# Ten running sums kept as halves: five in PSUM, five through three rotating banks, and a dot product that writes over its row

## The chip, the cores and the metric

The kernel runs on one core of a Trainium2 chip. The metric is device time in microseconds (us), the median of several runs. On the core, TensorE (PE in the profile) multiplies matrices and writes the products to PSUM, whose eight banks each hold a tile of 128 x 512 float32. VectorE (DVE) and ScalarE (ACT) read PSUM and SBUF, GpSimd (POOL) issues the indirect DMAs that fetch rows, and SyncE (SP) issues the others. Each engine runs its own instructions in order and waits on semaphores for the others.

## The reference

One layer of a diffusion backbone over 128 prompt tokens and 1024 sample tokens of width 1024, nine token tiles of 128 in all: norm, a mixer with a spatial gate and a two-way recurrence, a residual, and then PEER retrieval, where this change lies. Cut to that:

```python
def peer(x, w_q, sub_keys, u_tab, v_tab):        # 8 heads, 2 x 128 keys, 128*128 experts
    s = einsum('thpc,hpkc->thpk', q, sub_keys)   # scores of the two key halves
    ...                                          # 16 best of each half, 16 best sums of a head
    idx, g = chosen experts (128 a token), softmax over each head's 16
    a = gelu(einsum('bd,bed->be', x, u_tab[idx])) * g
    return einsum('be,bed->bd', a, v_tab[idx])
x = x + gate2 * peer(h, ...)                     # then a last norm and the store
```

## The kernel before

The first 1.78 ms norm the tokens, run the mixer in groups of token tiles, work out the experts of every token, and write a weight matrix G to DRAM for five of the tiles. The rest is retrieval, done in two ways at once.

**Dense.** The five tiles of `DENSE` (640 tokens) meet all 16384 experts, in 128 expert tiles of 128 (the loop over `e`). For one expert tile, `hidden` multiplies `u` with the tokens in two halves of 320 columns (`pH`, 24 matmuls each: 8 steps of the contraction, three products of split operands), ScalarE applies gelu into `a`, VectorE multiplies by G (`Gt`, line 1062), and the pair `split` makes `aH`, `aL` (line 99 on ScalarE, line 100 on VectorE). `u` and `v` are loaded and split in the same way. Then `a` times `v` is added to the sums, ten blocks of 128 tokens by 512 columns, three matmuls a block. Six blocks (three token tiles, `RES`) have a PSUM bank each for the whole loop and are added up there (`pout`, `out_res`). The other four (`ROT` = 2 tiles) are multiplied only after every fourth expert tile (`GI` = 4), for the four together (`prot`, `out_rot`: 12 matmuls a block); VectorE then adds the block to an SBUF sum `accd` (line 1045). 32 such groups make up the loop.

**Row by row.** The tiles of `GATHER` get their 128 chosen rows a token by indirect DMA. `gather` takes a row of `u` into a slot (`gu`), multiplies it by the token's vector with a running sum (line 798: the product goes to a scratch tile `jk`, the sum to `dots`), and after 16 of them fetches 16 rows of `v` (`gv`) and adds them up, weighted, in `acc` (line 813). This work fills VectorE beside the dense loop: `fill` is called after each split and each sum, advances `gather` by a fixed rate, and ties the new instructions behind an earlier one of the dense work (`anchor`, `paced`). The late choice of experts of a tile (`combine_late`, tile names `late`, `cmp`, `prod`) is filled in the same way.

PSUM is two rings: `pmm` (tag `mm`, six banks) and `ptp` (tag `tp`, two banks). A ring hands its banks out in the order of the code, so a new tile waits until the reader of the tile that had the bank before has finished. `pH`, `prot` and, before the dense loop, transposes, squares (`sqj`), the one-hot products of the G build (`pG`) and others all come from `tp`. What order an engine's instructions stand in is decided by a scheduler when the kernel is built; the code gives the dependencies.

At the end `final` multiplies a tile's sum by the gate, adds the residual, norms and stores it.

Of the kernel before, what the change touches and what calls it, by code (L numbers as in the profile page):

```python
# [20 lines left out]
NT = 9            # token tiles of 128: tile 0 is the prompt, 1..8 the sample  # L21
NS = 8
EPS = 1e-6
CF = {}           # slots of [128, 512] and of [128, 1024] in the pool of a phase
NGR = 4           # slots of fetched rows, and those that the dense pass adds
# [7 lines left out]
AH = (1, 2)       # of how many blocks of one-hots ScalarE does the weighting  # L33
# [4 lines left out]
TB = 32           # tokens of a block of the weight matrix in DRAM  # L38
OT = 4            # tokens of a block of one-hots
GI = 4            # expert tiles of one load of the weights  # L40
# units of 128 x 1024 weights in the stream
U_ZI, U_HG, U_GR = 0, 4, 16
GATHER = [0, 1, 2, 3]                             # token tiles whose experts are fetched row by row
DENSE = [5, 6, 7, 8, 4]                           # token tiles that meet every expert
ND = len(DENSE)
TD = 128 * ND
RES = 3                                           # dense tiles whose sums stay in PSUM
ROT = ND - RES


@with_exitstack
def hybrid_kernel(ctx, tc, x_all, pos, c2t, w_ada, b_ada, wst, wspt, bsp, lbraw, vecs, fng, skt, state,
# [8 lines left out]
    def pmm(name="pmm"):  # L61
        return psum.tile([128, 512], F32, name=name, tag="mm", bufs=6)

    def ptp(name="ptp"):
        return psum.tile([128, 512], F32, name=name, tag="tp", bufs=2)
# [3 lines left out]
    gate_d = dram.tile([4, D], F32, name="gate_d")      # gate1 (ctx, lat), gate2 (ctx, lat)  # L69
# [12 lines left out]
    vec = consts.tile([128, 24], F32, name="vec")        # g1(8) g2(8) sgu(4) hgrn(4), channel on partition  # L82
# [6 lines left out]
    lb = consts.tile([128, 3, 8], F32, name="lb")        # lb, (1-lb)/2, (1+lb)/2  # L89

# [13 lines left out]
    def anchor(ins, keep):  # L104
        """the filling work on VectorE queues behind the main stream's instruction `keep` anchors ago"""
        anchors.append(ins)
        while len(anchors) > keep:
            anchors.popleft()
# [15 lines left out]
    def mmx(ps, a, b, first, last):  # L124
        """a.T @ b for operands in one float32 part or in two float32r parts"""
# [10 lines left out]
    def rap(t, off, dims):  # L136
        """free-dim pattern on a tile"""
        a = t[:]
        return bass.AP(tensor=a.tensor, offset=a.offset + off, ap=[list(a.ap[0])] + dims)

# [9 lines left out]
    # work that fills the engines beside the main stream: generators, advanced a step at a time  # L150
# [42 lines left out]
    # order of the six modulation vectors: shift1 scale1 gate1 shift2 scale2 gate2  # L193
# [30 lines left out]
    def norm_T(pool, xn, which, cnd, parts, back=None):  # L224
        """transposes normalised tiles, applies scale and shift, stores the parts; back(k, full) sees
        the whole float32 value"""
# [41 lines left out]
    def proj_rows(u0, opd, n, evac, native, half=None):  # L268
        """token-major product with a 512 wide block (4 units); opd(k): parts [128, T]; evac(i, psum)"""
# [16 lines left out]
    def hgrn(pool, blocks, proj, vsrc, states):  # L286
        """blocks: (token tile, head) of each 128 columns; proj(j, evac): products for q, fw, bw"""
        NB = len(blocks)
        NTOK = NB * 128
        K2 = pool.tile([128, 2, NTOK], F32, name="K2")       # fw, bw  # L290
        Q2 = pool.tile([128, 2, NTOK], F32, name="Q2")       # bw, fw
        F2 = pool.tile([128, 2, NTOK], F32, name="F2")       # fw, bw
# [27 lines left out]
        for lev in range(7):  # L320
            w = 1 << lev
            Kc = pool.tile([128, NTOK], F32, name="Kc", bufs=1)   # even segments forward, odd ones backward
# [11 lines left out]
            # K: fw first halves by the total of the second, bw second halves by the total of the first  # L334
# [8 lines left out]
            # totals of the doubled segments: the second level in T2, the others in place of the gates  # L343
# [7 lines left out]
        T128 = tbase                                        # F2[:, d, T128 + block]  # L351
# [63 lines left out]
    def combine(gp, t, tv, ti, al=None, c4=None, V=V, h0=0, h1=8, res=None):  # L415
        """the 16 best sums of a head: products of the two lists, with (i+1)(j+1) <= 16"""
        if al is None:
            def al(name, n, dt=F32):
                return gp.tile([128, n], dt, name=name, bufs=1)
# [25 lines left out]
        if res is None:  # L445
            res = al("res", 384).rearrange("p (a b) -> p a b", a=3)    # i1, i2, g
# [3 lines left out]
        hk = lambda x: x[:, :, None, :].to_broadcast(SH)                     # over the list position  # L450
        lp = lambda x: x[:, :, :, None].to_broadcast(SH)                     # over the chosen
# [26 lines left out]
        # softmax over the 16 of a head  # L478
# [16 lines left out]
        else:  # L495
# [3 lines left out]
            rt = gp.tile([128, 2, 128], F16, name="rt", bufs=4)      # i2, i1  # L499
            V.tensor_copy(rt, pt[:, 0:256].rearrange("p (a b) -> p a b", a=2))  # L500
            rg = gp.tile([128, 128], F32, name="rg", bufs=4)         # g (scaled)
            V.tensor_scalar(rg, pt[:, 256:384], 16384.0, None, op0=OP.mult)
            gl = gp.tile([128, 2, 128], F16, name="gl", bufs=4)      # its float16 part, what is left
# [4 lines left out]
    def build_G(gp, i, rt, rg, gl, tags):  # L508
        SH = [128, 2, 128, OT]

        def one_hots(t0):
            o4 = gp.tile([128, 4, 128 * OT], F16, name="oh", tag="c4", bufs=3)
            oh = o4[:, 0:2].rearrange("p a (j t) -> p a j t", t=OT)          # of i2, of i1
# [673 lines left out]
```

## Time and profile before

| | |
|---|---|
| three runs | 3690.14, 3692.68, 3700.58 us |
| median | 3692.68 us |
| profiled execution | span 3697.6 us; the page gives no other time for it |
| PE busy in the span | 3351.2 us (91%) |
| VectorE busy | 2840.2 us (77%) |
| ScalarE busy | 1157.4 us (31%) |
| GpSimd busy | 1440.8 us (39%) |
| dense loop, first to last `pout` or `prot` | 1784.3 to 3674.2 us of the span |

The span reaches from the first to the last instruction. Matmuls overlap, each beginning before the one ahead of it has ended, so how fast PE goes is read from one start to the next, and its idle time from the rows that name a wait.

### The profile page before, as it was taken

To read this page: it belongs to the slowest core of one execution; us is meant where nothing else is said; L and a number is where in the kernel's file an instruction comes from. 1 tells how busy PE (TensorE), PEld (TensorE's weight loads), DVE (VectorE), ACT (ScalarE), POOL (GpSimd) and SP (SyncE) were. 2 spreads that over 40 slices of the span, in tenths; PEclk is the share of its full clock that TensorE was granted. 3 is DMA by queue.
4 is the path that set the end of the run, shared out by engine and by line. 5 is a ranking of instruction groups with operands and counts; after the bars stand their busy time and mean duration, and the time that the engine had idled before them with its cause. 6 is when DMAs were issued, how large, how long until landed. Compare 5 with 4: busy or idle time off the path is not lost. (4 is left out here: it accounts for less than half of the span.)

```text
span 3697.6 us, 48818 instructions
## 1 busy us (share of the span) xinstructions
PE 3351.2 (91%) x17547; PEld 2757.2 (75%) x17547; DVE 2840.2 (77%) x5427; ACT 1157.4 (31%) x2075; POOL 1440.8 (39%) x1128
## 2 busy tenths in 40 slices
PE   7787889899797899888789999889999989999997
PEld 3265678777476676576688989788888878898996
DVE  1315698787499987588787889888888888888888
ACT  2511233432222387735322222222222222222222
POOL 0100632265311220000255554556555465655664
PEclk9899999999898999888799999999999999999998
DMA  7676854488842476441798898889988799989986
GB/s 267 226 272 208 297 189 153 158 292 307 296 161 97 163 278 252 172 165 75 257 327 307 316 335 286 311 298 330 326 308 316 256 327 338 318 301 328 328 313 249
DMA packets 361957, 971.12 MB, mean 263 GB/s; under 512 B 32721, under 2 KB 142673, under 8 KB 356081
## 3 DMA queue, kind: packets, MB, share of 16 engines
q0 software_dynamic: 149824, 546.37, 41.6%
q1 hardware_dynamic: 211888, 421.62, 33.1%
q8 instruction: 138, 2.26, 0.2%
q14 instruction: 107, 0.87, 0.1%
HBM read 897.07 MB, written 70.80 MB: 262 GB/s over the span
## 5 line engine op out<-in xcount | busy, mean ns | idle before, releaser
L795 POOL DMA_INDIRECT gu<-in_urow_dram,ix x512 | 693.5, 1354 | 1024.8 <-DVE jk L798 368.8
L808 POOL DMA_INDIRECT gv<-in_vrow_dram,ix x512 | 694.7, 1357 | 720.6 <-DVE acc L813 388.2
L798 DVE SCALAR_TENSOR_TENSOR jk<-gu,h2r 128x1024 f16<-128x1024 f32 x512 | 624.9, 1220 | 125.0 <-DMA gu<-in_urow_dram,ix 118.7
L813 DVE SCALAR_TENSOR_TENSOR acc<-gv,act,acc 128x1024 f32<-128x1024 f32 x508 | 651.3, 1282 | 65.9 <-DMA gv<-in_vrow_dram,ix 57.9
L129 PE MATMUL pH<-h2DH,uH 128*128 128x320 f32 x2016 | 626.1, 311 | 11.3 <-DVE accd L1045 10.4
L131 PE MATMUL pH<-h2DH,uL 128*128 128x320 f32 x2016 | 623.6, 310 | 3.4 <-DVE uL L100 3.4
L130 PE MATMUL pH<-h2DL,uH 128*128 128x320 f32 x2016 | 624.2, 310 | 0.0
L129 PEld LDWEIGHTS pH<-h2DH,uH 128*128 128x128 f32 x2016 | 380.5, 189 | 21.8 <-DVE accd L1045 15.6
L130 PEld LDWEIGHTS pH<-h2DL,uH 128*128 128x128 f32 x2016 | 380.3, 189 | 4.4
L131 PEld LDWEIGHTS pH<-h2DH,uL 128*128 128x128 f32 x2016 | 380.1, 189 | 4.3 <-DVE uL L100 4.3
L129 PE MATMUL pout<-vH,aH 128*128 128x512 f32 x768 | 298.5, 393 | 22.6 <-ACT vH L99 16.3
L99 ACT ACTIVATE vH<-vr 128x1024 fp32r<-128x1024 f32 x128 | 133.3, 1058 | 561.4 <-DMA vr<-in_vrow_dram 289.4
L130 PE MATMUL pout<-vL,aH 128*128 128x512 f32 x768 | 301.1, 392 | 6.2 <-DVE vL L100 6.2
L131 PE MATMUL pout<-vH,aL 128*128 128x512 f32 x768 | 300.4, 391 | 1.1 <-DVE aL L100 1.0
L129 PE MATMUL prot<-vH,aH 128*128 128x512 f32 x512 | 211.7, 414 | 57.8 <-DVE accd L1045 51.8
L99 ACT ACTIVATE wH<-wraw 128x1024 fp32r<-128x1024 f32 x118 | 125.1, 1060 | 439.4 <-PE pq L130 148.4
L100 DVE TENSOR_TENSOR vL<-vr,vH 128x1024 fp32r<-128x1024 f32 x128 | 156.0, 1220 | 93.7 <-ACT vH L99 93.6
L99 ACT ACTIVATE aH<-a 128x640 fp32r<-128x640 f32 x128 | 94.2, 736 | 368.5 <-DVE a L1062 363.7
L130 PE MATMUL prot<-vL,aH 128*128 128x512 f32 x512 | 208.0, 406 | 0.0
L131 PE MATMUL prot<-vH,aL 128*128 128x512 f32 x512 | 207.3, 405 | 0.0
L99 ACT ACTIVATE uH<-ur 128x1024 fp32r<-128x1024 f32 x126 | 133.4, 1058 | 234.1 <-PE pH L130 214.5
L543 PE MATMUL pG<-oh 128*128 128x128 f16 x1280 | 159.4, 281 | 35.0 <-ACT Gs L546 20.3
(343 smaller groups left out, 6407.7 us busy)
## 6 DMA issues: line engine op xcount, KB each, us to landing
wraw<-in_wst_dram SPq DMA_DIRECT2D x216, 512.0 KB, 4.4
vr<-in_vrow_dram SPq DMA_DIRECT2D x128, 512.0 KB, 6.4
ur<-in_ut_dram SPq DMA_DIRECT2D x126, 512.0 KB, 6.8
G_d<-Gs SPq DMA_DIRECT2D x40, 1024.0 KB, 4.1
Gt<-G_d SPq DMA_DIRECT2D x160, 256.0 KB, 8.7
wraw<-in_w_ada_dram SPq DMA_DIRECT2D x48, 512.0 KB, 4.4
gu<-in_urow_dram,ix POOLq DMA_INDIRECT x512, 6.3
gv<-in_vrow_dram,ix POOLq DMA_INDIRECT x512, 6.9
```

Of the source, the lines that this page charges most:

```text
L99: A.activation(H, src, AF.Copy)
L100: return V.tensor_tensor(out=L, in0=src, in1=H.bitcast(F32), op=OP.subtract)
L129: P.matmul(ps, a[0], b[0], start=first, stop=False)
L130: P.matmul(ps, a[0], b[1], start=False, stop=False)
L131: P.matmul(ps, a[1], b[0], start=False, stop=last)
L543: P.matmul(pg[:, tt * 128:(tt + 1) * 128], oh[:, 0, :, tt], og[a][:, :, tt], start=(a == 0), stop=(a == 1))
L795: G.indirect_dma_start(out=ur, out_offset=None, in_=urow, in_offset=bass.IndirectOffsetOnAxis(ap=ix[:, c:c + 1], axis=0))
L798: paced(V.scalar_tensor_tensor(jk, ur, 1.0, h2r, op0=OP.mult, op1=OP.mult, accum_out=dots[:, k:k + 1]))
L808: G.indirect_dma_start(out=vr, out_offset=None, in_=vrow, in_offset=bass.IndirectOffsetOnAxis(ap=ix[:, c:c + 1], axis=0))
L813: paced(V.scalar_tensor_tensor(acc, vr, act[:, k:k + 1], acc, op0=OP.mult, op1=OP.add))
```

## The change

PSUM's eight banks are cut five and three in place of six and two: `mm` gets five, `tp` three. The unit of a sum becomes a half tile. The first five halves stay in PSUM (two tiles and the left half of the third), five rotate, and `accd` is five tiles of 128 x 512 in place of two of 128 x 1024. A group thus has 15 `pout` matmuls an expert tile (18 before), 60 `prot` matmuls (48 before) and five sums on VectorE (four before). The rate of `fill` is divided by 3 x 4 + 5 = 17 calls a group in place of 16, so that a group still fetches 24.4 rows. The final takes a tile's sum as two halves for all five tiles, into a `ftmp` tile each. The product of line 798 goes back over the fetched row in float32, and the scratch tile `jk` (float16) is gone. Comments are dropped, which moves line numbers by one or so.

```diff
-RES = 3
-ROT = ND - RES
+RES = 5
+ROT = 2 * ND - RES
...
-        return psum.tile([128, 512], F32, name=name, tag="mm", bufs=6)
+        return psum.tile([128, 512], F32, name=name, tag="mm", bufs=5)
...
-        return psum.tile([128, 512], F32, name=name, tag="tp", bufs=2)
+        return psum.tile([128, 512], F32, name=name, tag="tp", bufs=3)
...
-                jk = gat.tile([128, D], F16, name="jk", bufs=1)
-                paced(V.scalar_tensor_tensor(jk, ur, 1.0, h2r, op0=OP.mult, op1=OP.mult,
+                paced(V.scalar_tensor_tensor(ur, ur, 1.0, h2r, op0=OP.mult, op1=OP.mult,
                                              accum_out=dots[:, k:k + 1]))
...
-    po = [[pmm("pout") for _ in range(2)] for _ in range(RES)]
-    accd = [dp.tile([128, D], F32, name=f"accd{i}") for i in range(ROT)]
+    halves = [(i, n) for i in range(ND) for n in range(2)]
+    po = [pmm("pout") for _ in range(RES)]
+    accd = [dp.tile([128, 512], F32, name=f"accd{i}") for i in range(ROT)]
...
-        advance(gather_q, RATE[4] * GI / (3 * GI + 2 * ROT))
+        advance(gather_q, RATE[4] * GI / (3 * GI + ROT))
...
+    def cols(i, n):
+        return slice(i * 128, (i + 1) * 128), slice(n * 512, n * 512 + 512)
...
+        for z in range(RES):
+            t, s = cols(*halves[z])
+            mmx(po[z], [aH[:, t], aL[:, t]], [vH[:, s], vL[:, s]], e == 0, e == 127)
...
+        for z in range(ROT):
+            t, s = cols(*halves[RES + z])
+            pr = ptp("prot")
+            for m, (_, aH, aL, vH, vL) in enumerate(grp):
+                mmx(pr, [aH[:, t], aL[:, t]], [vH[:, s], vL[:, s]], m == 0, m == len(grp) - 1)
+            if grp[0][0] == 0:
+                ins = V.tensor_copy(accd[z], pr)
+            else:
+                ins = V.tensor_tensor(out=accd[z], in0=accd[z], in1=pr, op=OP.add)
+            fill(ins)
...
+    sums = po + accd
...
-        final(dp, DENSE[i], dst, po[i] if i < RES else [dst], x1, gt2, fgd)
+        final(dp, DENSE[i], dst, sums[2 * i:2 * i + 2], x1, gt2, fgd)
```

The first place is VectorE's queue at the sums of one group in the middle of the dense loop, where the second row by row tile has just been finished. `jk` or `gu` is a product of line 798, `accd` a sum, and the waits in brackets are on DMAs (DMASW, DMAHW), PE, ScalarE (Activation), GpSimd (Pool) or VectorE's own last results (DVE). Before:

```order
L798 SCALAR_TENSOR_TENSOR jk_19331,dots_19318<-gu_19329,h2r_19315 128x1024 [waits DMASW5_49]
L798 SCALAR_TENSOR_TENSOR jk_19335,dots_19318<-gu_19333,h2r_19315 128x1024 [waits DMASW6_49,DVE_49]
L1045 TENSOR_TENSOR accd0_13757<-accd0_13757,prot_19365 128x512 [waits PE_49]
L798 SCALAR_TENSOR_TENSOR jk_19345,dots_19318<-gu_19343,h2r_19315 128x1024 [waits DMASW7_49,DVE_49]
L1045 TENSOR_TENSOR accd0_13757<-accd0_13757,prot_19387 128x512 [waits PE_49]
L798 SCALAR_TENSOR_TENSOR jk_19381,dots_19318<-gu_19379,h2r_19315 128x1024 [waits DMASW2_49,DVE_49]
L798 SCALAR_TENSOR_TENSOR jk_19385,dots_19318<-gu_19383,h2r_19315 128x1024 [waits DMASW0_49,DVE_49]
L1045 TENSOR_TENSOR accd1_13758<-accd1_13758,prot_19405 128x512 [waits PE_49]
L798 SCALAR_TENSOR_TENSOR jk_19403,dots_19318<-gu_19401,h2r_19315 128x1024 [waits DMASW1_49,DVE_49]
L100 TENSOR_TENSOR vL_19524<-vr_19521,vH_19523 128x1024 [waits DMAHW5_49,Activation_49]
L798 SCALAR_TENSOR_TENSOR jk_19421,dots_19318<-gu_19419,h2r_19315 128x1024 [waits DMASW3_49,DVE_49]
L1045 TENSOR_TENSOR accd1_13758<-accd1_13758,prot_19427 128x512 [waits PE_49]
```

Four sums stand there with one or two products between them. The same place of the changed kernel:

```order
L797 SCALAR_TENSOR_TENSOR gu_19082,dots_19081<-gu_19082,h2r_19078 128x1024 [waits DMASW4_49]
L797 SCALAR_TENSOR_TENSOR gu_19085,dots_19081<-gu_19085,h2r_19078 128x1024 [waits DMASW5_49]
L1044 TENSOR_TENSOR accd0_13628<-accd0_13628,prot_19112 128x512 [waits PE_49]
L797 SCALAR_TENSOR_TENSOR gu_19126,dots_19081<-gu_19126,h2r_19078 128x1024 [waits DMASW7_49]
L797 SCALAR_TENSOR_TENSOR gu_19129,dots_19081<-gu_19129,h2r_19078 128x1024 [waits DMASW2_49,DVE_49]
L1044 TENSOR_TENSOR accd1_13629<-accd1_13629,prot_19132 128x512 [waits PE_49]
L797 SCALAR_TENSOR_TENSOR gu_19146,dots_19081<-gu_19146,h2r_19078 128x1024 [waits DMASW0_49]
L1044 TENSOR_TENSOR accd2_13630<-accd2_13630,prot_19149 128x512 [waits PE_49]
L797 SCALAR_TENSOR_TENSOR gu_19163,dots_19081<-gu_19163,h2r_19078 128x1024 [waits DMASW1_49]
L797 SCALAR_TENSOR_TENSOR gu_19166,dots_19081<-gu_19166,h2r_19078 128x1024 [waits DMASW3_49,DVE_49]
L1044 TENSOR_TENSOR accd3_13631<-accd3_13631,prot_19169 128x512 [waits PE_49]
```

The fifth sum follows one product later; the density of sums and products is about the same, and most products no longer wait on VectorE itself.

The second place is a little ahead of it in the changed kernel, where the products of one head are fetched. GpSimd issues the fetches in this order:

```order
L795 DMA gu_18478<-in_urow_dram,ix1_13750 128x1024
L795 DMA gu_18481<-in_urow_dram,ix1_13750 128x1024
L795 DMA gu_18563<-in_urow_dram,ix1_13750 128x1024
L795 DMA gu_18572<-in_urow_dram,ix1_13750 128x1024
L795 DMA gu_18581<-in_urow_dram,ix1_13750 128x1024
```

and VectorE works on them in this one (rows of other work between them included):

```order
L797 SCALAR_TENSOR_TENSOR gu_18563,dots_18371<-gu_18563,h2r_13752 128x1024 [waits DMASW3_49]
L100 TENSOR_TENSOR uL_18569<-ur_18566,uH_18568 128x1024 [waits DMAHW4_49,PE_49]
L100 TENSOR_TENSOR vL_18578<-vr_18575,vH_18577 128x1024 [waits DMAHW1_49,Activation_49]
L1061 TENSOR_TENSOR a_18505<-a_18505,Gt_18499 128x640 [waits DMAHW6_49,DMAHW7_49,DMAHW5_49,Activation_49]
L797 SCALAR_TENSOR_TENSOR gu_18581,dots_18371<-gu_18581,h2r_13752 128x1024 [waits DMASW5_49,DVE_49]
L100 TENSOR_TENSOR aL_18560<-a_18505,aH_18559 128x640 [waits Activation_49]
L797 SCALAR_TENSOR_TENSOR gu_18572,dots_18371<-gu_18572,h2r_13752 128x1024 [waits DMASW4_49]
```

The row fetched fourth is used after the one fetched fifth. Over the whole program such a step back occurs 112 times in the changed kernel and 42 times in the one before.

## Rows read from the trace of the kernel before

**Rows 1.** Page: its header, and PE's granted clock in tenths over 40 slices.

```profile
span 3697.6 us, 48818 instructions
...
PEclk9899999999898999888799999999999999999998
```

**Rows 2.** Windows: busy of PE, PEld, DVE, ACT, POOL; PEclk, DMA, GB/s.

```profile
1784.00:3674.60 1890.60, 1804.24 (x9888) 1625.04 (x9888) 1578.32 (x2126) 460.75 (x673) 1058.21 (x776) 0.98 0.88 311
...
2200.00:2400.00 200.00, 188.11 (x1021) 169.78 (x1020) 175.62 (x297) 48.27 (x69) 112.62 (x82) 0.96 0.86 306
...
3400.00:3600.00 200.00, 199.84 (x1132) 182.38 (x1131) 167.80 (x196) 52.22 (x77) 120.52 (x85) 1.00 0.91 321
```

**Rows 3.** PE's groups in the dense loop: busy, mean ns | idle before.

```profile
L129 PE MATMUL pH<-h2DH,uH 128*128 128x320 f32 x2016 | 626.1, 311 | 11.3 <-DVE accd L1045 10.4 <-ACT a L981 0.8
...
L129 PE MATMUL pout<-vH,aH 128*128 128x512 f32 x768 | 298.5, 393 | 22.6 <-ACT vH L99 16.3 <-ACT aH L99 6.2
L129 PE MATMUL prot<-vH,aH 128*128 128x512 f32 x512 | 211.7, 414 | 57.8 <-DVE accd L1045 51.8 <-DVE accd L1043 4.1 <-ACT a L981 1.7
```

**Rows 4.** Timeline of PE: start, us, operation [idle before <-releaser].

```profile
1836.51 0.79 PE L129 MATMUL prot<-vH,aH 128*128 128x512 f32 x1 [4.10 <-DVE accd L1043]
...
2440.92 0.39 PE L130 MATMUL prot<-vL,aH 128*128 128x512 f32 x1
2441.15 0.39 PE L131 MATMUL prot<-vH,aL 128*128 128x512 f32 x1
2450.73 0.80 PE L129 MATMUL prot<-vH,aH 128*128 128x512 f32 x1 [9.19 <-DVE accd L1045]
...
2531.26 0.31 PE L129 MATMUL pH<-h2DH,uH 128*128 128x320 f32 x1
2531.41 0.31 PE L130 MATMUL pH<-h2DL,uH 128*128 128x320 f32 x1
...
3395.53 0.60 PE L129 MATMUL prot<-vH,aH 128*128 128x512 f32 x1 [2.98 <-DVE accd L1045]
```

**Rows 5.** Timeline of DVE in the longest stall.

```profile
2440.05 1.22 DVE L798 SCALAR_TENSOR_TENSOR jk<-gu,h2r 128x1024 f16<-128x1024 f32 x1 [4.54 <-DMA gu<-in_urow_dram,ix]
...
2449.99 0.68 DVE L1045 TENSOR_TENSOR accd<-accd,prot 128x512 f32<-128x512 f32 x1
...
2451.74 0.68 DVE L1045 TENSOR_TENSOR accd<-accd,prot 128x512 f32<-128x512 f32 x1
```

**Rows 6.** DVE's groups in the dense loop.

```profile
L798 DVE SCALAR_TENSOR_TENSOR jk<-gu,h2r 128x1024 f16<-128x1024 f32 x384 | 468.7, 1221 | 85.0 <-DMA gu<-in_urow_dram,ix 79.7
...
L1045 DVE TENSOR_TENSOR accd<-accd,prot 128x512 f32<-128x512 f32 x123 | 83.6, 680 | 5.3 <-PE prot L131 5.3
```

**Rows 7.** Timeline of DVE in a run of row products.

```profile
2535.98 1.23 DVE L798 SCALAR_TENSOR_TENSOR jk<-gu,h2r 128x1024 f16<-128x1024 f32 x1
...
2537.24 1.23 DVE L798 SCALAR_TENSOR_TENSOR jk<-gu,h2r 128x1024 f16<-128x1024 f32 x1
...
2538.40 1.22 DVE L100 TENSOR_TENSOR vL<-vr,vH 128x1024 fp32r<-128x1024 f32 x1
```

**Rows 8.** PE's groups ahead of the dense loop.

```profile
L543 PE MATMUL pG<-oh 128*128 128x128 f16 x1280 | 159.4, 281 | 35.0 <-ACT Gs L546 20.3 <-ACT sqj L248 10.5 <-ACT oh L520 2.5
...
L232 PE MATMUL pnt<-ident,xr 128*128 128x128 f32 x72 | 17.9, 370 | 21.1 <-ACT xr L252 12.7 <-ACT sqj L248 7.4 <-ACT full L237 0.7
```

**Rows 9.** Timeline of ACT in the last build of G.

```profile
1757.85 1.28 ACT L520 ACTIVATE oh<-oh,rg 128x128 f16<-128x128 f16 x4
1759.02 1.96 ACT L546 ACTIVATE Gs<-pG 128x256 f32<-128x256 f32 x4
1760.74 1.30 ACT L520 ACTIVATE oh<-oh,rg 128x128 f16<-128x128 f16 x4
```

**Rows 10.** Timeline of DVE at the end.

```profile
3675.74 0.67 DVE L1045 TENSOR_TENSOR accd<-accd,prot 128x512 f32<-128x512 f32 x1
...
3689.22 1.28 DVE L833 SCALAR_TENSOR_TENSOR accd<-accd,rstd,fgd 128x1024 f32<-128x1024 f32 x1 [0.72 <-POOL rstd L95]
```

More of the change, by code (lines that the diff above doesn't have):

```diff
@@ L1025, in load_split @@
         return H, L
+    def cols(i, n):
+        return slice(i * 128, (i + 1) * 128), slice(n * 512, n * 512 + 512)
     def out_res(e, aH, aL, vH, vL):
-        for i in range(RES):
-            t = slice(i * 128, (i + 1) * 128)
-            for n in range(2):
-                s = slice(n * 512, n * 512 + 512)
-                mmx(po[i][n], [aH[:, t], aL[:, t]], [vH[:, s], vL[:, s]], e == 0, e == 127)
-    def out_rot(grp):
-        for i in range(ROT):
-            t = slice((RES + i) * 128, (RES + i + 1) * 128)
-            for n in range(2):
-                s = slice(n * 512, n * 512 + 512)
-                pr = ptp("prot")
-                for m, (_, aH, aL, vH, vL) in enumerate(grp):
-                    mmx(pr, [aH[:, t], aL[:, t]], [vH[:, s], vL[:, s]], m == 0, m == len(grp) - 1)
-                if grp[0][0] == 0:
-                    ins = V.tensor_copy(accd[i][:, s], pr)
-                else:
-                    ins = V.tensor_tensor(out=accd[i][:, s], in0=accd[i][:, s], in1=pr, op=OP.add)
-                fill(ins)
+        for z in range(RES):
+            t, s = cols(*halves[z])
+            mmx(po[z], [aH[:, t], aL[:, t]], [vH[:, s], vL[:, s]], e == 0, e == 127)
+    def out_rot(grp):
+        for z in range(ROT):
[8 more added lines that the diff above has]
+            fill(ins)
     grp = []
@@ L1078, in hybrid_kernel @@
     nc.sync.dma_start(fgd, fng[None].to_broadcast([128, D]))
+    sums = po + accd
     for i in range(ND):
-        dst = accd[i - RES] if i >= RES else dp.tile([128, D], F32R, name="ftmp", tag="vL", bufs=GI + 1).bitcast(F32)
+        dst = dp.tile([128, D], F32R, name="ftmp", tag="vL", bufs=GI + 1).bitcast(F32)
         x1 = dp.tile([128, D], F32, name="x1", tag="raw", bufs=3)
-        final(dp, DENSE[i], dst, po[i] if i < RES else [dst], x1, gt2, fgd)
+        final(dp, DENSE[i], dst, sums[2 * i:2 * i + 2], x1, gt2, fgd)
     advance(gather_q, 10000)
```

## The prediction, made blind

> **What bounds the kernel now.** I read the page's header first: a span of 3697.6 us [rows 1], 5 above the median of the three runs. The profiled execution has no other time, so changes are summed against its span and then taken off the median, 3692.7. PE's clock, in tenths over forty slices, is near full except around slices 16 to 19, where the queries and the last weight matrix are worked out [rows 1].
>
> Then the windows. From 1784 to 3674.6, just over half of the span, PE is busy 1804 of 1891 us with 9888 matmuls, VectorE 1578 [rows 2]. At full rate a 512-column matmul starts 0.227 us after the one before, a 320-column one 0.147, averaged over runs of which a pair each stands in [rows 4]. With 3840 and 6048 of them that is 871 + 887 = 1758 us. So the loop is PE's, and 132 us are lost: 86 of idle time and 46 in which matmuls were slower than at the full clock (granted 0.98). A stretch without idle shows the full pace to be reachable: 1132 matmuls in 200 us at clock 1.00, with VectorE at 168 and the DMA engines at 0.91 [rows 2]. A stretch with the late choice of experts shows less room: VectorE 176 while PE has 188 [rows 2].
>
> Where the idle time is, PE's groups say. The 512 first matmuls of a `prot` quadruple waited 51.8 us on the sums of line 1045 and 4.1 on those of line 1043, those of `pH` another 10.4; with 2.5 us on ScalarE's read of a bank that makes 68.8 us waiting for a `tp` bank [rows 3]. `pout` has 22.5 us of waits on operands, 16.3 of it at the loop's opening [rows 3].
>
> Why VectorE is late can be read in the longest stall. PE's last matmul of a second half starts at 2441.15, its next at 2450.73 [rows 4]. VectorE had waited 4.5 us for a fetched row until 2440.05, then worked off its queue, and came to the first sum at 2449.99 and the second at 2451.74 [rows 5]. VectorE has time enough overall; it is late by bursts, and two banks give it little leeway: half three takes the bank of half one, so the first sum has to end within one half of 12 matmuls, 2.72 us.
>
> **The change, part by part.**
>
> *The third bank.* Half four, not half three, now waits for the first sum: due two halves after its own half, 5.44 us. The third sum is due when the next `pH` begins, again two halves on. Each deadline moves by 2.72 us, and a stall that comes from lateness shrinks by at most that, once a group. I read PE's starts group by group (start to start, less 0.227): 17 of the 32 groups stall at a bank, the first at 1836.51, the last at 3395.53, the longest 9.35 us before 2450.73 [rows 4]. They sum to 73 us, a little over the 68.8 since a first slow matmul is counted too. Ten exceed 2.72 and lose that, 27.2 us; seven are shorter and go, 13.2 together. That is **-40**. Bounds: 0, if VectorE becomes later by as much as it is allowed to, and -69, if it catches up always.
>
> *The clock.* Of the 46 us of slow matmuls most follow stalls. Ten stalls remain, in shorter form, and keep most of their slow stretch; seven go and three come under 1 us. I take a fifth, **-9** (bounds 0 and -46).
>
> *The fifth sum.* Matmuls stay 30 an expert tile: 15 `pout` and 15 `prot` in place of 18 and 12, so PE's work is unchanged. VectorE gets one sum a group more, 32 in all, each 0.68 us long [rows 6] and about 0.60 from start to start: +19 us on VectorE. The row products at each sum drop from 1.53 to 1.44, so sums and products together take less of the 2.72 us between halves, about 2.4. A group's rows stay 24.4.
>
> *The product over its row.* The fetched slot came free at the end of this instruction before and does so now; the fetch's wait is the same. The float16 `jk` cost 1.22 us [rows 6], a float32 result of that shape (`vL` [rows 7]) 1.22: nothing. What goes is a wait: `jk` had one slot, so a product behind a product waited for the first to be written. Products start 1.26 us apart, but 1.16 before other work [rows 7]. In the dense loop's order 163 products stand right behind another and wait on VectorE; in the new order 45 do. 118 x 0.11 = **-13** on VectorE, bounds 0 and -13. The 0.11 may be the read of the running sum, not the wait; then nothing is saved (a rival below).
>
> By the Trainium skill ("VectorE: DVE Perf Modes", section "The DRAIN you can't avoid") an operation waits for the pipe to empty whether or not it waits on a semaphore, so that fewer waits gain nothing and only the count of operations tells. The trace so far speaks against it, with 1.26 where there is a wait and 1.16 where there is none.
>
> So VectorE's load grows by 6 us of its 312 idle (1891 - 1578). In a stalled group the sums are late by 0.2 us more: 10 x 0.2 = **+2**.
>
> *Ahead of the loop.* `tp` serves transposes, squares and the G build there. PE waited 20.3 us for `Gs` to be read, 10.5 and 7.4 for squares [rows 8]. The first hardly counts: in the last build ScalarE runs without a gap, two blocks in 2.89 us [rows 9], and a bank more doesn't shorten its work. The squares stand in chains of norms, where PE's wait is partly another's. I take -8 of 18. The ring `mm` with five banks costs where a four-tile product follows another, five places, one read of a bank each at most (0.68, the sum's [rows 6]): +3. Together **-5**, bounds +3 and -38.
>
> *The end.* From the last sum at 3675.74 to the last product of the norm at 3689.22 [rows 10] VectorE works off finals. Three more short operations stand behind the last sum; the two more `ftmp` tiles take slots that the last group's matmuls free by then: **+1**.
>
> Sum: -40 - 9 + 2 - 5 + 1 = -51. Taken off the median: **3641 us**.
>
> **The rivals.**
>
> *The third bank takes nearly all* (0.17). If VectorE's bursts are mostly under two halves once it can run behind, the bank waits (69), their slow stretches (35) and 18 ahead of the loop go: 122 us, less the 6 for the added work, 3577, and 3560 to 3613 as a range. For it: the stretch without idle runs at full pace with VectorE at 84%. Against: ten stalls are longer than 2.72, and the bursts come from fetched rows, which more banks do not bring earlier.
>
> *VectorE only gets later* (0.18). PE's stalls let VectorE catch up; without them the lateness is carried into the next operands. In the stretch with the late choice VectorE has 12% left at PE's pace there and under 7% at full pace [rows 2], and the fifth sum takes one of them. The waits then turn up at `pout` and `pH`, for `aL`, `vL` and `uL`, and the time is 3668 to 3704, around 3685.
>
> *The dropped waits give nothing back* (half, whatever else happens). VectorE's load then grows by 19 us, not 6, the sums are 0.6 us later a group, and the stalled groups give back 6 us, not 2: 3645, within the forecast's own range. This is what the Trainium skill's DRAIN section of that page would have.
>
> *Rows used out of order* (0.10, slower). Without `jk` nothing holds the products in the order of their fetches: the queue steps back 112 times, 42 before. VectorE then stands at a row not yet landed while another lies ready, and the slot of that one, still full, holds up GpSimd's next fetch. Waits for rows of `u` are 79.7 us in the loop now [rows 6]; if each of 70 more steps costs the time of a product, 1.22 [rows 6], that is 85 us more, all at the products that stand among the sums. If the banks pass on all of it, the time is 3641 + 85 = 3726; it decides from 62 us, what the forecast gains and 0.3% on top: 3704 to 3730. Against it: the steps are mostly by one or two rows, and six slots lie between fetch and use.
>
> *The forecast itself* (0.55): 3613 to 3668.
>
> **How the numbers follow.** A change under 0.3%, 11 us, cannot be told from none here: 3682 to 3704. Below it lie the forecast (0.55), the case of all stalls (0.17) and a third of the late case (0.06): 0.78. The rest of the late case, 0.12, is within; the out-of-order case, 0.10, slower. For 8 in 10, I cut the low case at 3585 (0.07 below) and the high ones at 3700 (0.12 above): **3585 to 3700**.
>
> **What the new profile would show.** If right: waits of `prot` and `pH` on the sums fall from 66 us to 25 or so, most stalled groups have none, PE busy in the loop stays near 1795 while the loop shortens to some 1842 us; 160 sums at 0.68; products behind products at 1.15 to 1.16; ScalarE's back-to-back build and the 23 us behind PE's last matmul are as they were. If the waits for rows of `u` rise well above 80 us, or `pout` waits on `aL` and `vL` by tens of us, a rival is at work. What I know least is how long a burst of VectorE lasts once PE no longer waits for it; if they lengthen with the leeway, the gain is half.

## The result, and the profile after

The changed kernel is slower: 3802.2 us, median of four runs (3788.6 to 3812.6), against 3693.7 of the kernel before (3690.1 to 3700.6). The ratio is 1.028, 95% interval 1.026 to 1.031. The forecast of 3641 and its range up to 3700 are both wrong. The profiled run took 3788.6 us and its span is 3786.8, so a run's time is its span and 1.8 us.

The windows of the changed kernel, over its dense loop (columns as in [rows 2]):

```profile
1760.80:3760.60 1999.80, 1838.98 (x9888) 1640.01 (x9888) 1584.45 (x2156) 455.55 (x672) 1062.25 (x776) 0.97 0.85 294
```

The loop begins 23 us earlier than before, at 1760.8, and takes 1999.4 us from its first to its last `prot`, 110 more. Against the 1758 us of full pace, 161 us are idle (86 before) and 81 are slower matmuls (46 before). So 75 of the 110 us are new waits, and 35 are matmuls slower than at the full clock (granted 0.97, 0.98 before). VectorE's work is up by 6 us, 1584 for 1578 [rows 2], as forecast.

PE's groups on the page of the changed kernel (all of them lie in the dense loop) answer to [rows 3]:

```profile
L131 PE MATMUL pH<-h2DH,uL 128*128 128x320 f32 x2016 | 623.6, 310 | 10.5 <-DVE uL L100 10.4
L129 PE MATMUL pH<-h2DH,uH 128*128 128x320 f32 x2016 | 625.2, 310 | 6.9 <-DVE accd L1044 5.1
...
L129 PE MATMUL prot<-vH,aH 128*128 128x512 f32 x640 | 264.1, 413 | 81.8 <-DVE accd L1044 71.3
...
L129 PE MATMUL pout<-vH,aH 128*128 128x512 f32 x640 | 258.6, 408 | 51.6 <-ACT aH L99 34.8
L131 PE MATMUL pout<-vH,aL 128*128 128x512 f32 x640 | 260.5, 407 | 23.7 <-DVE aL L100 22.6
```

The waits for a bank did not fall: `prot` and `pH` together wait 88.7 us, 69.1 before, although there is a bank more. And the operands are late too: `aH` holds up `pout` for 34.8 us (6.2 before), `aL` for 22.6 and `uL` for 10.4. `aH` is ScalarE's, but made from VectorE's `a`. All of it points at VectorE, and VectorE's groups in the dense loop say what VectorE waits for (compare [rows 6]):

```profile
L812 DVE SCALAR_TENSOR_TENSOR acc<-gv,act,acc 128x1024 f32<-128x1024 f32 x381 | 488.8, 1283 | 23.9 <-DMA gv<-in_vrow_dram,ix 18.4
L797 DVE SCALAR_TENSOR_TENSOR gu<-gu,h2r 128x1024 f32<-128x1024 f32 x384 | 462.3, 1221 | 215.2 <-DMA gu<-in_urow_dram,ix 205.7 <-issue 8.5
...
L1044 DVE TENSOR_TENSOR accd<-accd,prot 128x512 f32<-128x512 f32 x154 | 104.8, 681 | 1.9 <-PE prot L131 1.9
```

The line for rows of `v` in the kernel before:

```profile
L813 DVE SCALAR_TENSOR_TENSOR acc<-gv,act,acc 128x1024 f32<-128x1024 f32 x381 | 488.7, 1283 | 27.0 <-DMA gv<-in_vrow_dram,ix 19.7
```

Waits for rows of `u` went from 79.7 to 205.7 us, those for rows of `v` hardly moved (19.7 to 18.4). The products now write `gu`, and as the second place of the built order had shown, VectorE no longer uses the rows in the order in which GpSimd fetches them. What that does is plain in the worst place. GpSimd's timeline of the changed kernel there:

```profile
2619.10 1.68 POOL L795 DMA_INDIRECT gu<-in_urow_dram,ix  x1 [2.63 <-DVE gu L797]
...
2623.37 0.94 POOL L795 DMA_INDIRECT gu<-in_urow_dram,ix  x1 [0.30 <-issue]
2624.61 0.94 POOL L795 DMA_INDIRECT gu<-in_urow_dram,ix  x1 [0.30 <-issue]
2629.27 1.28 POOL L807 DMA_INDIRECT gv<-in_vrow_dram,ix  x1 [3.72 <-DVE gu L797]
2633.03 1.68 POOL L795 DMA_INDIRECT gu<-in_urow_dram,ix  x1 [2.48 <-DVE gu L797]
...
2642.60 0.94 POOL L807 DMA_INDIRECT gv<-in_vrow_dram,ix  x1 [6.66 <-DVE gu L797]
```

VectorE's timeline of the same stretch:

```profile
2631.53 1.22 DVE L797 SCALAR_TENSOR_TENSOR gu<-gu,h2r 128x1024 f32<-128x1024 f32 x1
2632.67 0.08 DVE L797 DVE_READ_ACCUMULATOR gu<-gu,h2r 128x1 f32 x1
2632.67 1.22 DVE L797 SCALAR_TENSOR_TENSOR gu<-gu,h2r 128x1024 f32<-128x1024 f32 x1
2633.82 0.08 DVE L797 DVE_READ_ACCUMULATOR gu<-gu,h2r 128x1 f32 x1
2641.10 1.23 DVE L797 SCALAR_TENSOR_TENSOR gu<-gu,h2r 128x1024 f32<-128x1024 f32 x1 [7.20 <-DMA gu<-in_urow_dram,ix]
...
2646.48 1.22 DVE L797 SCALAR_TENSOR_TENSOR gu<-gu,h2r 128x1024 f32<-128x1024 f32 x1
2647.63 0.08 DVE L797 DVE_READ_ACCUMULATOR gu<-gu,h2r 128x1 f32 x1
2647.63 0.68 DVE L1044 TENSOR_TENSOR accd<-accd,prot 128x512 f32<-128x512 f32 x1
```

and PE's:

```profile
2648.37 0.50 PE L129 MATMUL prot<-vH,aH 128*128 128x512 f32 x1 [3.70 <-DVE accd L1044]
```

Going by the two queues' orders, the row that VectorE stands at until 2641.10 was fetched at 2633.03. Four rows fetched before it, at 2619.10, 2623.37, 2624.61 and 2629.27, lie unused all that time; they are used at 2646.48, 2648.23, 2649.97 and 2651.71. Their slots stay taken, so after one more fetch at 2635.01 GpSimd in turn stands, 6.66 us, until VectorE has used the late row; its next fetch is at 2642.60. The sum that PE needs is queued behind, and PE stands 3.70 us at `prot`. In the code the late row and the one fetched after it stand ahead of the rows fetched from 2621.08 to 2629.27, so GpSimd's queue has left the code's order as VectorE's has. Counted against the code over the whole program, GpSimd's fetches step back 62 times and VectorE's uses 85 times in the changed kernel; in the one before it was 22 and 23.

Pairing every fetch of the loop with its use, 768 rows in each kernel, gives the size. "Ahead" is a row used while one that was fetched earlier is still unused; the waits are VectorE's for the landing of these rows.

| | rows ahead | waits at them, us | rows in order | waits at them, us |
|---|---|---|---|---|
| before | 58 | 63.5 | 710 | 35.9 |
| changed | 197 | 206.4 | 571 | 17.7 |

139 more rows are taken ahead, and VectorE waits 143 us more at such rows, about a microsecond each. In the changed kernel VectorE waited 0.27 us on average at a row ahead of one other, 1.08 at one ahead of two, 2.36 of three and 3.05 of four.

### The profile page after: what moved, and what is told of

Its sections match the earlier page's. It is cut to its first block, busy times and chain, and to the rows that moved or that the text cites. A ratio compares the mean times of both kernels' runs of the same rounds, so it can differ in the third digit from the quotient of the medians.

```text
span 3786.8 us, 48520 instructions
## 1 busy us (share of the span) xinstructions
PE 3383.5 (89%) x17547; PEld 2771.7 (73%) x17547; DVE 2845.7 (75%) x5461; ACT 1147.9 (30%) x2075; POOL 1444.7 (38%) x1128
## 5 line engine op out<-in xcount | busy, mean ns | idle before, releaser
L807 POOL DMA_INDIRECT gv<-in_vrow_dram,ix x512 | 711.1, 1389 | 859.0 <-DVE acc L812 426.8
L797 DVE SCALAR_TENSOR_TENSOR gu<-gu,h2r 128x1024 f32<-128x1024 f32 x512 | 617.4, 1221 | 258.1 <-DMA gu<-in_urow_dram,ix 247.9
L131 PE MATMUL pH<-h2DH,uL 128*128 128x320 f32 x2016 | 623.6, 310 | 10.5 <-DVE uL L100 10.4
L129 PE MATMUL prot<-vH,aH 128*128 128x512 f32 x640 | 264.1, 413 | 81.8 <-DVE accd L1044 71.3
L129 PE MATMUL pout<-vH,aH 128*128 128x512 f32 x640 | 258.6, 408 | 51.6 <-ACT aH L99 34.8
L131 PE MATMUL pout<-vH,aL 128*128 128x512 f32 x640 | 260.5, 407 | 23.7 <-DVE aL L100 22.6
L130 PE MATMUL prot<-vL,aH 128*128 128x512 f32 x640 | 260.5, 407 | 0.0
L131 PE MATMUL prot<-vH,aL 128*128 128x512 f32 x640 | 259.6, 406 | 0.0
L130 PE MATMUL pout<-vL,aH 128*128 128x512 f32 x640 | 256.7, 401 | 3.0 <-DVE vL L100 3.0
L129 PEld LDWEIGHTS prot<-vH,aH 128*128 128x128 f32 x640 | 127.4, 199 | 119.2 <-DVE accd L1044 80.8
L129 PEld LDWEIGHTS pout<-vH,aH 128*128 128x128 f32 x640 | 124.8, 196 | 78.9 <-ACT aH L99 41.2
```

What stands on the lines that cost most here:

```text
L129: P.matmul(ps, a[0], b[0], start=first, stop=False)
L130: P.matmul(ps, a[0], b[1], start=False, stop=False)
L131: P.matmul(ps, a[1], b[0], start=False, stop=last)
L797: paced(V.scalar_tensor_tensor(ur, ur, 1.0, h2r, op0=OP.mult, op1=OP.mult, accum_out=dots[:, k:k + 1]))
L807: G.indirect_dma_start(out=vr, out_offset=None, in_=vrow, in_offset=bass.IndirectOffsetOnAxis(ap=ix[:, c:c + 1], axis=0))
```

## Experiments

My theory A was that the order in which rows are used makes the loss, and the banks bring little. Rival B: the banks and the fifth sum make the loss.

**The product over its row alone**, in the kernel before:

```diff
-                jk = gat.tile([128, D], F16, name="jk", bufs=1)
-                paced(V.scalar_tensor_tensor(jk, ur, 1.0, h2r, op0=OP.mult, op1=OP.mult,
+                paced(V.scalar_tensor_tensor(ur, ur, 1.0, h2r, op0=OP.mult, op1=OP.mult,
```

> The kernel before with one edit: the product goes over its fetched row and the scratch tile is gone; PSUM and the sums are as before. Theory A (without the scratch tile the products leave the order of their fetches, and VectorE stands at rows not yet landed): the loss is here, and the gain of the banks (23 us ahead of the dense loop, up to 50 in it) is not, so 3800 to 3875 us, waits of products for fetched rows near 200 us or more in the dense loop. Theory B (the halves, the fifth sum or the three and five banks cost it): no change, 3680 to 3705, those waits near 80.

Measured: 3839.7 us, ratio 1.038 (1.035 to 1.042). Its VectorE group for these products in the loop:

```profile
L797 DVE SCALAR_TENSOR_TENSOR gu<-gu,h2r 128x1024 f32<-128x1024 f32 x384 | 461.6, 1221 | 253.1 <-DMA gu<-in_urow_dram,ix 252.7
```

209 rows are used ahead. This part alone loses more than the whole change, so the banks and the fifth sum aren't needed for the loss.

**The banks alone**: the changed kernel with the scratch tile back, of one byte an element. Room for it is made by keeping the weights of the rows (`ga`) in float16.

```diff
-            ga = gat.tile([128, 128], F32, name=f"ga{t}")
+            ga = gat.tile([128, 128], F16, name=f"ga{t}")
...
-                paced(V.scalar_tensor_tensor(ur, ur, 1.0, h2r, op0=OP.mult, op1=OP.mult,
+                jk = gat.tile([128, D], U8, name="jk", bufs=1)
+                paced(V.scalar_tensor_tensor(jk, ur, 1.0, h2r, op0=OP.mult, op1=OP.mult,
```

> The changed kernel with the scratch tile of the product back (of one byte an element, and the weights of the fetched rows in float16, since there is no room for the old one): halves, rings and sums as changed, products in the old order. Theory A: the gain of the banks alone, 3620 to 3675 us, waits of products for rows near 80 in the dense loop. Theory B: as slow as the changed kernel, 3780 to 3815.

Measured: 3688.6 us, ratio 0.9985 (0.997 to 1.000). PE's groups in its dense loop:

```profile
L129 PE MATMUL pH<-h2DH,uH 128*128 128x320 f32 x2016 | 627.2, 311 | 8.1 <-DVE accd L1045 7.0 <-ACT uH L99 1.1
...
L131 PE MATMUL pH<-h2DH,uL 128*128 128x320 f32 x2016 | 625.2, 310 | 6.4 <-DVE uL L100 6.4
L129 PE MATMUL prot<-vH,aH 128*128 128x512 f32 x640 | 256.6, 401 | 42.9 <-DVE accd L1045 34.6 <-ACT a L981 6.7 <-DVE accd L1043 1.4
...
L131 PE MATMUL pout<-vH,aL 128*128 128x512 f32 x640 | 254.0, 397 | 14.0 <-DVE aL L100 13.7
L129 PE MATMUL pout<-vH,aH 128*128 128x512 f32 x640 | 253.7, 401 | 26.9 <-ACT vH L99 16.7 <-ACT aH L99 9.8 <-issue 0.3
...
L130 PE MATMUL pout<-vL,aH 128*128 128x512 f32 x640 | 252.9, 395 | 1.9 <-DVE vL L100 1.9
```

The groups of the kernel before that stand beside these and aren't in [rows 3]:

```profile
L131 PE MATMUL pH<-h2DH,uL 128*128 128x320 f32 x2016 | 623.6, 310 | 3.4 <-DVE uL L100 3.4
L130 PE MATMUL pout<-vL,aH 128*128 128x512 f32 x768 | 301.1, 392 | 6.2 <-DVE vL L100 6.2
L131 PE MATMUL pout<-vH,aL 128*128 128x512 f32 x768 | 300.4, 391 | 1.1 <-DVE aL L100 1.0
```

And the window over its dense loop:

```profile
1771.40:3661.40 1890.00, 1806.57 (x9888) 1627.31 (x9888) 1590.06 (x2154) 457.05 (x672) 1062.15 (x776) 0.98 0.89 311
```

The banks' waits fall from 69 to 51 us, and those for operands (`pout`, and `uL` at `pH`) rise from 33 to 49. The loop takes 1889.9 us, to a tenth what it took before. What the third bank gave, VectorE's lateness took back at the next operand: my rival of the lateness. What is left is that the loop began 13 us earlier; by medians it is 4 to 6 us, which can't be told from none. The range that I had set for theory A, 3620 to 3675, is missed, since it counted on a gain of the banks in the loop. Rival B is out.

**Order restored.** Three kernels tie each use of a row behind the one before it in the code, with a dependency that sets the queue's order and adds no wait:

```diff
+    rowins = []
+    def behind(ins):
+        if rowins:
+            tc.add_manual_dep(ins.ins, rowins[0].ins.name,
+                              mybir.DependencyInfo(mybir.DependencyClass.NoSync, mybir.DependencyReason.DATA),
+                              reason="rows in the order of their fetch")
+        rowins[:] = [ins]
...
                 paced(ins)
+                behind(ins)
```

The first does so for the products of the changed kernel, the second for its products and its weighted sums of `v` rows, the third for both in the kernel before.

> The changed kernel with one order more for the scheduler: each product stands behind the product of the row before it in the code, without a wait. Theory A: like the changed kernel with its scratch tile, 3620 to 3675 us; if the dropped waits of VectorE on itself are worth something, some 5 us less than that kernel. Theory B: 3780 to 3815.

> As the one with products in order, and the weighted sums of the rows of v are in the same chain, so that VectorE takes all rows in the order of the code. 26 places are left in the one before where a product of the next head goes ahead of a sum. Theory A, if any step back costs: a little less again, 3600 to 3670. If only runs of steps among products cost: the same as the products in order within 0.3%. Theory B: 3780 to 3815.

> The kernel before, banks, sums and scratch tile as they were, with all rows taken in the order of the code. In its dense loop 58 rows were taken ahead of one fetched earlier and still unused, here 6. Theory A (each such row costs VectorE about 1.05 us of waiting, and the loop passes most of it on): waits for rows fall from 99 to about 45 us, the loop by 30 to 45, 3645 to 3665 us. Rival (the order helps only where the third bank lets PE run on): 3680 to 3705.

Measured: 3694.4 us (ratio 0.9995, 0.998 to 1.001), 3645.7 (0.986, 0.983 to 0.989) and 3652.2 (0.9875, 0.986 to 0.989). One dependency that orders the products takes back the whole loss: 58 rows of the loop are ahead again, and VectorE waits 61.7 us at them. The time lies above theory A's 3620 to 3675, as with the banks alone. The products' groups of the three pages (over the whole program; there the kernel before has 118.7 us of waits for rows of `u`, the changed one 247.9), first with the products in order,

```profile
L806 DVE SCALAR_TENSOR_TENSOR gu<-gu,h2r 128x1024 f32<-128x1024 f32 x512 | 611.1, 1220 | 135.5 <-DMA gu<-in_urow_dram,ix 132.8
```

then with all rows in order,

```profile
L806 DVE SCALAR_TENSOR_TENSOR gu<-gu,h2r 128x1024 f32<-128x1024 f32 x512 | 610.1, 1221 | 97.0 <-DMA gu<-in_urow_dram,ix 95.8
```

and in the kernel before with all rows in order:

```profile
L807 DVE SCALAR_TENSOR_TENSOR jk<-gu,h2r 128x1024 f16<-128x1024 f32 x512 | 625.6, 1222 | 72.1 <-DMA gu<-in_urow_dram,ix 65.4
```

The dependency is on the uses alone, and GpSimd's fetches follow: against the code they step back 62 times in the changed kernel, 21 times with the products in order and 4 times with all rows. Ordering all rows leaves 8 rows ahead in the changed kernel and 6 in the one before, and both then beat the kernel before: its own order, with 58 rows ahead, had cost it some 45 us (1.25%); its loop goes from 1890 to 1836. With all rows in order the changed kernel and the one before can't be told apart.

**Two banks, and pairs swapped.** Both start from the changed kernel with all rows in order. The one goes back to rings of six and two, the other uses each pair of `u` rows second first, so that half of these rows are one place ahead.

```diff
-        return psum.tile([128, 512], F32, name=name, tag="tp", bufs=3)
+        return psum.tile([128, 512], F32, name=name, tag="tp", bufs=2)
...
-                ins = V.scalar_tensor_tensor(ur, ur, 1.0, h2r, op0=OP.mult, op1=OP.mult,
+                for z in (1, 0):
+                    ins = V.scalar_tensor_tensor(two[z], two[z], 1.0, h2r, op0=OP.mult, op1=OP.mult,
```

> The changed kernel with all rows in order, and the rings back at six and two: halves and five sums on two rotating banks. If the third bank is worth what the trace of before said (2.72 us off each stall) once the rows are in order: 25 to 50 us more in the dense loop and 10 to 20 ahead of it, 3680 to 3715 us. If it is worth something only ahead of the loop: 3655 to 3668.

> The changed kernel with all rows in a set order in which each pair of products stands the wrong way round: the second of two fetched rows of u first. 190 rows of the dense loop are then taken ahead of the one before them, as many as in the changed kernel (197), but by one place only. Theory A1 (a row taken ahead costs about 1 us however little it is ahead): waits for rows near 200 us, 3780 to 3830 us. Theory A2 (only rows taken several places ahead cost, since the fetch of the neighbour lands soon after): waits below 120 us, 3640 to 3700.

Measured: 3690.7 us (0.998, 0.996 to 1.000) and 3703.2 (1.002, 1.000 to 1.004). With two banks the loop takes 1866.9 us for 1856.4 with three and begins 16 us later: third bank and early start are worth 26 us in the profiled pair of spans (3681.9 and 3655.5), 45 by medians. The time is in the range expected of a bank that helps in the loop, but the loop gives only 10 us of it in this pair, where I had expected 25 to 50. The swapped pairs put 190 rows ahead, all but one by one place. VectorE waits 0.46 us at each, and the loop is 35 us longer than with all rows in order. 190 rows a microsecond each would have been 190 us. So swaps of neighbours are cheap and the long jumps are dear; a price for each row whatever its distance doesn't hold. The time is 3 us above the range for that case, and the loop begins 16 us later than in the kernel it starts from (1788.7 and 1772.5); why, no run here shows.

**Over the row with all in order, and the rings switched.** The first is the ordered kernel before, with the product over its row as in the first experiment. The second is the ordered kernel before with rings of five and three up to the loop, and of six and two in it.

```diff
-        return psum.tile([128, 512], F32, name=name, tag="mm", bufs=6)
+        return psum[0].tile([128, 512], F32, name=name, tag="mm", bufs=psum[1])
...
+    psum_a.close()
+    psum[:] = [ctx.enter_context(tc.tile_pool(name="psumd", bufs=1, space=bass.MemoryType.PSUM, reuse_waits="tile")), 6, 2]
```

> The kernel before with all rows in order and the product over its row (no scratch tile): between the kernel before in order (3652 us, its loop 1836) and halves on two banks in order (3691, loop 1867). If the five halves and their fifth sum make the difference: as the kernel before in order, 3645 to 3660, loop near 1836. If the product over its row does, even in order: 3675 to 3695, loop near 1865.

> The kernel before with all rows in order and the PSUM rings five and three up to the dense loop, six and two in it. If the third bank's gain lies ahead of the loop only (the loop began 12 to 24 us earlier with it, and was no shorter): the loop begins near 1772 and takes 1836, 3630 to 3640 us. If the earlier start is given back at the loop's opening or by waits for the switch: 3648 to 3660.

Measured: 3676.6 us (0.996, 0.994 to 0.997) and 3629.0 (0.983, 0.980 to 0.985). The rings, switched where the loop begins, start it 20 us earlier at no cost. But with the product over its row the ordered kernel is 24 us slower by medians (0.8% by the two ratios), with 6 rows ahead in both, and that left a question: the write over the row, or the wait that left with the scratch tile?

**Two scratch slots, and a wait put back.** The first is the ordered kernel before with two slots of scratch, of one byte, so that a product need not wait for the one right before it. The second writes over the row and makes each product wait for the one before.

```diff
-                jk = gat.tile([128, D], F16, name="jk", bufs=1)
+                jk = gat.tile([128, D], U8, name="jk", bufs=2)
...
-                behind(ins)
+                behind(ins, mybir.DependencyClass.Sync if k else mybir.DependencyClass.NoSync)
```

> The kernel before with all rows used in the order of their fetch (3652 us, ratio 0.9875), with a scratch tile of one byte an element and two slots in place of the float16 one with one slot: a product no longer waits for the product right before it, but still doesn't write over its row. In order, writing over the row was 24 us slower than the scratch tile. Theory 1 (it is the writing over the fetched row that costs): the time stays within 6 us of 3652, the waits of products for rows of u near 33 us, a row's fetch on GpSimd's queue near 1364 ns. Theory 2 (it is the products that stand closer and so run into rows that haven't landed): 3670 to 3682, the waits for rows of u near 49, a fetch near 1440 ns.

> The kernel before with all rows used in the order of their fetch and the product written over its row (3677 us, ratio 0.9956), but each product is made to wait for the one before it, as the scratch tile of one slot had made it. Theory 1 (writing over the fetched row costs): the time stays at 3671 to 3683, a fetch on GpSimd's queue near 1440 ns. Theory 2 (the wait between products was worth something): it comes back to within 6 us of 3652, waits for rows of u near 33 us, a fetch near 1364 ns. A time between the two ends says that each has a share.

Measured: 3684.6 us (0.996, 0.995 to 0.998; 3 above the range of its theory 2) and 3649.6 (0.987, 0.985 to 0.989). It isn't the write over the row: with two scratch slots every engine's queue is that of the eighth kernel, only the products' output differs, and so is the time (0.996 both). It is the dependency between neighbouring products, whatever they write to. But its removal does two things: it takes a wait off the chip, and it makes the scheduler build another queue. With the dependency 204 products stand right behind another, and 10 runs are of five; without, 275 and 17.

**A given queue.** The kernel of the eighth experiment (over the row, in order, no wait), with VectorE's queue fixed instruction by instruction to that of the kernel with the wait; PE's, GpSimd's and SyncE's queues then come out the same too, and ScalarE's but for four places. `QUEUE` holds the numbers of VectorE's instructions in that order, each as the difference from the last. Then, with the edit of the eleventh, the changed kernel with both things restored, order and wait.

```diff
+    for step in QUEUE:
+        n += step
+        ins = every.get(f"I-{n}")
...
+            tc.add_manual_dep(ins.ins, last.ins.name,
+                              mybir.DependencyInfo(mybir.DependencyClass.NoSync, mybir.DependencyReason.DATA),
+                              reason="a given queue")
```

> In order and written over the row, the products cost 25 us less with a wait between them (3650 us, ratio 0.9868) than without (3677, 0.9956). With the wait, 204 products stand right behind another on VectorE's queue, and 10 runs of five; without it 275, and 17 runs of five. This kernel has no wait between the products, and VectorE's queue is given row by row as in the kernel with the wait. Theory 1 (the place in the queue costs: the scheduler bunches products that nothing keeps apart): 3640 to 3658, waits for rows of u near 33 us. Theory 2 (the wait itself is worth it on the chip, by spacing the products): 3668 to 3684, waits for rows near 49.

> The changed kernel with all rows used in the order of their fetch (3646 us, ratio 0.9863), and each product made to wait for the one before it. If order and the wait are all that the product over its row had taken away, the changed kernel with both is 25 us faster than with order alone, some 3621 (3610 to 3632), level with or below the version with rings switched (3629). If the five halves and three banks have a cost of their own once the rows are in order, it stays above 3636.

Measured: 3655.7 us (0.989, 0.987 to 0.991) and 3628.1 (0.981, 0.979 to 0.983). The windows over the dense loops of four kernels, the eighth (over the row, in order), the eleventh (with the wait), the twelfth and the thirteenth, each in a fence of its own:

```profile
1786.80:3647.90 1861.10, 1794.44 (x9888) 1618.70 (x9888) 1569.10 (x2122) 461.41 (x672) 1096.15 (x776) 0.98 0.90 316
```

```profile
1793.40:3632.00 1838.60, 1786.74 (x9886) 1616.84 (x9887) 1580.78 (x2122) 461.31 (x672) 1059.80 (x776) 0.99 0.90 320
```

```profile
1790.70:3620.50 1829.80, 1784.31 (x9888) 1617.69 (x9888) 1568.99 (x2122) 461.99 (x672) 1095.25 (x776) 0.99 0.91 321
```

```profile
1770.80:3601.30 1830.50, 1786.28 (x9888) 1613.30 (x9888) 1591.42 (x2154) 456.72 (x672) 1078.84 (x776) 0.99 0.91 321
```

With the same queue and no wait VectorE is 12 us less busy (1569 for 1581), and the time is that of the kernel with the wait, within the intervals. With another queue and as little work for VectorE the loop takes 31 us more. So the place in the queue costs, not the wait or its lack. That it is the longer runs of products that do it (the waits for rows of `u` in the loop are 49.0 us in the eighth, 29.1 in the twelfth) fits, but no run here changes the runs alone: between the eighth and the twelfth PE's queue differs as well.

The last kernel is the changed kernel as one would keep it: 1.9% faster than the kernel before, level with the rings switched, and 4.6% faster than the changed kernel (by the two ratios, 0.981 / 1.028 = 0.954).

## Why the prediction was wrong, step by step

**The step that failed is the product over its row**, which I costed as "nothing" but a dropped wait. The order had been seen: it is the last rival, at 0.10. I priced it by 70 more steps back in the whole program, at 1.22 us each, and judged that "the steps are mostly by one or two rows". One step back lets several rows pass, though. In the loop 139 more rows were used ahead, and VectorE waited 143 us more at such rows. Mostly by one or two rows is true, 157 of the 197, but a row two places ahead already cost 1.08 us, and the 40 that were three or four places ahead took half of the waiting, at 2.4 to 3.1 us each. "Six slots lie between fetch and use" was no argument against, since an unused row in its slot is what stops GpSimd. That rival's mechanism was right, and its price, 85 us, too low; its own range ended at 3730. First and third experiments show it: +147 us with the product over its row alone, and nothing left of the loss when the products are in order.

**The third bank, -40, and the clock, -9**, didn't come. With the banks alone the loop was as long as before, the waits having moved to `aL`, `aH` and `uL`, as the rival of the lateness said. Once all rows are used in order and the products wait, five halves on three banks are worth 6 us of loop (1830 us against 1836 for the ordered kernel before), which one profile of each doesn't tell from none. The time in slow matmuls went with the stalls, as I had it, but both grew: the idle time from 86 to 161 us, the slow matmuls from 46 to 81.

**The fifth sum and the dropped waits** were right in their sum, and that by luck. VectorE's work in the loop rose by 6 us, the difference of 19 and 13 that I had. But with the banks alone, which keep the waits, it rose by 12 (1590 for 1578), so the fifth sum took 12 and the dropped waits gave 6. In another queue they give more: the given queue, with the same 384 products in the same places, has VectorE 12 us less busy without the waits. They bring no time. The rival of the dropped waits was thus right on the time, but not on VectorE's load, which it let grow by 19. A product that doesn't wait starts 1.14 us after the one before it, 2631.53 to 2632.67 in the stretch above (1.26 in [rows 7] with the wait). The Trainium skill's rule ("VectorE: DVE Perf Modes", section "The DRAIN you can't avoid"), that taking away semaphores gains nothing, agrees with the time here, though not with VectorE's own pace. And only a wait for the very product before costs VectorE this: with two scratch slots a product waits for the one two products back, and still starts 1.14 us after its neighbour (2463.70 and 2464.84 in that kernel's trace).

**Ahead of the loop** -5 was too small: the loop began 23 us earlier in the changed kernel, 13 with the banks alone, 20 with the rings switched. PE's waits ahead of the loop in the changed kernel (total us, times, longest), to be read against [rows 8]:

```profile
PE pG L543 <- ACT Gs L546: 10.5, 16, 2.6
...
PE pG L543 <- ACT oh L520: 9.4, 14, 1.9
...
PE pG L543 <- ACT sqj L248: 0.4, 1, 0.4
```

The wait for `Gs`, which I took for nothing since ScalarE has no gap in the last build, fell from 20.3 to 10.5, and that for squares from 10.5 to 0.4. Part of it came back at the operand, as in the loop: the wait for `oh`, which ScalarE makes too, rose from 2.5 to 9.4. These three make 13 us of the 23; the rest I did not part. The gain lay within my bounds, and I had let only 8 of the 38 us count.

**The end** took 26.6 us from the last `prot` to the span's end (23.4 before): +3 for the +1.

Taken together: in its profiled run the changed kernel lost 110 us in the loop and 3 at the end, and gained 23 ahead of it, 89 in all, which is the difference of the two spans. By medians the loss is 109: the profiled run lies 14 us under the median of its kernel, and the profiled run before 6 above.

## What to carry to other kernels

Before you remove a scratch tile or another shared buffer, ask what order it holds up: a one-slot scratch, useless by its content, was what kept a queue of products nearly in the order of their fetches. Where rows stream through a ring of slots, compare the order of fetches on the one queue with that of uses on the other, count the rows that pass others and by how far, and state the order in the code rather than leave it to a dependency that is there for another reason. And give a bank to the stretch in which a bank is what is missing: in the loop here the third one only moved the wait while rows were out of order, and brought some 10 us (one pair of profiles) once they were in order, while ahead of the loop the same bank brought 13 to 23 us, in all kernels but the one with the pairs swapped.

## What the runs showed that I had not expected

- The wait at a row used ahead rose with the distance: 0.27, 1.08, 2.36 and 3.05 us for one to four places in the changed kernel. It isn't a fixed price: one place was 0.46 with the pairs swapped.
- A dependency on VectorE's uses alone brought GpSimd's fetches back into order as well: 62 steps back against the code in the changed kernel, 4 with all uses in order.
- Orders alone, at equal work on every engine, made 31 us of a loop of 1861 (eighth and twelfth kernels), and the wait that had seemed to matter made none.
- The kernel before had itself used 58 rows out of order, and ordering them alone brings 1.25% (ratio 0.9875).
